# An encoder layer on one core: sums of squares, weight sums and the Fourier fold take other places in the order

## The chip, the cores and the metric

The kernel runs on 1 core of one Trainium2 chip. The metric is the device time of one execution in microseconds, lower is better. The engines are PE (TensorE, the matmuls), DVE (VectorE), ACT (ScalarE), POOL (GpSimd) and SP (SyncE, which issues most transfers). Each engine works through its own list in the order in which the program wrote it, and waits at an instruction until what it needs is there.

## The reference

One encoder layer for 1024 prompt tokens and 256 sample tokens, all in fp32:

```
trunk(x):
  xn = rms_norm(x);  h = xn @ w_in              # u_f 256, c_q 384, c_kv 256, k_rope 64
  y_f = real(fft2(u_f))                         # over tokens and over 4 groups of 64
  q  = rms_norm(c_q) @ w_q_up;  kv = rms_norm(c_kv) @ w_kv_up   # 6 heads
  y_a = softmax(q k^T) v                        # rope on a part of q and k
  x = x + concat(y_f, y_a) @ w_out
  x = x + (silu(rms_norm(x) @ w_gate) * (rms_norm(x) @ w_up)) @ w_down   # 2816 wide
  return rms_norm(x)
```

## The kernel before

The tokens lie in three chunks: 0 and 1 are the prompt (512 columns each), 2 is the sample (256). A matrix product runs as three fp32r passes over a high and a low part of both operands (mm3, L112). A high part is a copy by ACT (L93), a low part a subtraction by DVE or POOL (L98). The order on PE, ACT, DVE and POOL is written out by hand: nothing is moved by a scheduler, so a line that stands elsewhere in the program stands elsewhere in each engine's list. Buffers come from rotating pools, and a matmul waits until a PSUM bank is free (four banks of kind mm, two double banks sc).

A sum of squares over the 1024 rows is an accumulator on which POOL adds squares that ACT made. The class Rstd turns it into a reciprocal root: pre splits the accumulator (ACT high part, DVE low part, tile ssq), mid sums it over the partitions with two matmuls (L188, L189) and takes logarithm and exponential on ACT, post is four DVE operations (post_op 0 to 3, L208 to L215); post_op 0 is the last to read the bank.

Stages, with their places in the profiled execution:

- 0 to 124: phase_A projects a chunk into the latents, proj_U into u_f and k_rope, in the order chunk 0, 2, 1. x_pre, x_mid and x_post make the root of the input norm, c_pre, c_mid and c_post those of the two latent norms, c_norm scales a latent. rcols (L410) transposes the root of the input norm and is needed behind proj_U.
- 124 to 169: the queries (q_rope, whose result two to three DVE operations read out of the bank, L578 and L581; q_nope), first keys (kproj) and the latent norms of chunk 1. fold_U, on DVE, folds u_f for the Fourier transform: its first call is four additions (L391), each other call four more operations.
- 169 to 199: the first four score blocks (step), with queries and values between them. From 199 on the folded u_f is used; then the attention, to about 450.
- 450 to 570: the output projection (out_proj, index m from 0 to 7 per chunk), with squares for the second norm in hacc, one accumulator for each chunk.
- 570 to 1136: gate and up projections, for chunks 0 and 1 as a block scheme with seven products in place of eight: it needs sums of weight blocks (S1 to S4, made in prep from the raw weights) and sums of activation blocks (T1 to T4, from scaled, the normalised rows of chunk 1, L1111, and C0, those of chunk 0). The products are started by run in the order of seq; chunk 2 goes the plain way (rest). The first pair of weights (fp 0) has its own order: A11, A12, A21, A22 first, then S2, S1, S3, S4, A22.
- From 1136 on: the down projection and the last norm.

Of the kernel before, what the change touches and what calls it, by code (L numbers as in the profile page):

```python
# [35 lines left out]
def encoder_kernel(ctx, tc, A, out):  # L36
# [425 lines left out]
    def step0(k):  # L462
        if k + 2 < KD:
            load_w(k + 2)
            load_x(0, k + 2)
        if k + 1 < KD:
            split_w(k + 1, 0)
            split_x(0, k + 1, nc.vector)
        split_w(k, 1)
        if k == KD - 2:  # L470
            for kk in range(4):
                load_x(2, kk)
        if k == KD - 1:
            x_pre(0)
            for kk in range(4, KD):
                load_x(2, kk)

    phase_A(0, {k: (lambda k=k: step0(k)) for k in range(KD)})
    proj_U(0, 0)
    x_mid(0)  # L480
    x_post(0)
    late_consts()
    proj_U(0, 1)
# [3 lines left out]
    evac_U(0, 1)  # L487
    for k in range(KD):
        split_x(2, k, nc.vector)
    c_pre(0)  # L490
    proj_U(0, 2)
    evac_U(0, 2)
    proj_U(0, 3)
# [3 lines left out]
    def hooks2(k):  # L497
        load_x(1, k)
        if k == 0:
            x_pre(2)  # L500
        if k == 2:
            c_mid(0)
        if k == 3:
            c_post(0)
            x_mid(2)
        if k == 4:
            x_post(2)
        if k >= 3:
            c_norm(0, k - 3)

    phase_A(2, {k: (lambda k=k: hooks2(k)) for k in range(KD)})
    evac_A(2)
# [3 lines left out]
    rcols(2)  # L516
    evac_U(2, 0)
    c_pre(2)
    proj_U(2, 1)
    evac_U(2, 1)  # L520
    rope_k(2)
# [15 lines left out]
            x_pre(1)  # L537

    phase_A(1, {k: (lambda k=k: hooks1(k)) for k in range(KD)})
    proj_U(1, 0)  # L540
    x_mid(1)
    x_post(1)
    W.split(2)
    proj_U(1, 1)
# [414 lines left out]
    q_rope(0, 0)  # L959
    q_nope(0, 0)  # L960
    q_rope(0, 2)
    c_mid(1)
    q_nope(2, 0)
    q_rope(1, 0)
    cch[1][0].post()
    q_nope(0, 1)
    q_rope(1, 2)
    c_norm(1, 0)
# [15 lines left out]
    qsplit(0, 0, 0)  # L984
    qsplit(0, 0, 1)
    W.split(5)
    fold_U(0, nc.vector)
    q_nope(1, 1)
    q_rope(2, 1)
    fold_U(1, nc.vector)  # L990
    W.split(6)
    kr_transpose(1)
    q_nope(1, 2)
    kproj(0, 1)
    q_nope(2, 2)
    fold_U(2, nc.vector)
    fold_U(3, nc.vector)
    W.split(ib + 1)
    more = [(t, h) for h in range(3, H) for t in (0, 2, 1)]
    vp = [(t, j) for t in range(3) for j in range(TC[t][1] // P)]  # L1000
    for s in range(4):
        step(S[s], extra.get(s, ()))
        if s == 3:
            W.split(ib + 2)
            step(None)
        for a in more[9 * s // 4 : 9 * (s + 1) // 4]:
            q_nope(*a)
        vproj(0, *vp[s])
        if s == 0:
            fold_U(4, nc.vector)  # L1010
    W.split(ib + 3, 0)

    R, Rh = [], {}
# [119 lines left out]
        scaled(C0[m], m, 0)  # L1133

    def parts0(m):
        B["B21" if m > 3 else "B11"][m % 4] = split(pair(512, "b"), C0[m], nc.gpsimd if m > 3 else nc.vector)

    def plain2(m):

# [32 lines left out]
            src = A["w_up" if q % 2 else "w_gate"]  # L1172
            raws2[q] = [wload(src[f_ * P : (f_ + 1) * P, :], 1024) for f_ in (q // 2 * 2, q // 2 * 2 + 1)]

    def prep(upto, only_sums=False):


        while done[0] < min(upto, len(seq)):
            n = done[0]
            fp, k, name = seq[n]  # L1180
            q = 2 * fp + k
            load_pair(q)
            ra, rb = raws2[q]
            blk = {"A11": ra[:, :512], "A12": ra[:, 512:], "A21": rb[:, :512], "A22": rb[:, 512:]}
            blk |= {"S3": blk["A11"], "S1": blk["A21"], "S4": blk["A12"], "S2": sums.get(q)}
            eng = nc.vector if fp else nc.gpsimd

            def made(o, x, y, op):
                eng.tensor_tensor(blk[o], blk[x], blk[y], op=op)

            if name == "S2" and q not in sums:
                made("S3", "A11", "A21", ALU.subtract)
                made("S1", "A21", "A22", ALU.add)
                blk["S2"] = sums[q] = tmp([P, 512])
                made("S2", "A22", "S3", ALU.subtract)
                blk["S2"] = sums[q]
                if fp == 0:
                    made("S4", "A12", "S2", ALU.subtract)
            elif name == "S4" and fp:
                made("S4", "A12", "S2", ALU.subtract)  # L1200
            if only_sums:
                return
            if n % 2 == 0:
                piece["tile"] = wtile([P, 2, 2, 512], F32R, "wo")
            o = piece["tile"][:, n % 2]
            piece[n] = split((o[:, 0], o[:, 1]), blk[name], nc.gpsimd if n > 7 else nc.vector)
            done[0] += 1
            if name == "A22" and (fp or n > 8):
                load_pair(q + 2)

    state = {}

# [89 lines left out]
    for m in range(9):  # L1302
        W.split(min(io + 8 + m + 3, idn))
        if m == 6:
            prep(4)
        if m == 7:
            prep(8)
        if m < 8:
            load_res(m + 1, 1) if m < 7 else None
            load_res(m, 2)  # L1310
            out_proj(W.get(io + 8 + m), m, 1)
        if m == 7:
            hch[1] = Rstd(hacc[1], 512, D)
            hch[1].pre()
            prep(9, True)
        if m == 8:
            hch[1].mid()
        if m > 0:
            out_proj(W.get(io + 7 + m), m - 1, 2)
            plain2(m - 1)  # L1320
        if m == 0:
            hch[0].mid()
            hch[0].post()
        elif m < 5:
            chunk0(m - 1)
            chunk0(m + 3)
        for k in {4: (0,), 5: (1,), 6: (2,), 7: (3, 4, 5, 6, 7)}.get(m, ()):
            parts0(k)
        if m == 5:
            load_pair(0)  # L1330
            load_pair(1)
    hch[1].post()


    run(0)
# [2 lines left out]
        scaled(B["T3"][j][1], j, 1)  # L1338
        scaled(B["B22"][j][1], j + 4, 1)
    run(1)  # L1340
    hch[2] = Rstd(hacc[2], 256, D)
    hch[2].out = r2
    hch[2].pre()
    prep(10)

    def combine(o, x, y):
# [2 lines left out]
    for j in range(4):  # L1349
        ca, cb = B["T3"][j][1], B["B22"][j][1]  # L1350
        B["T1"][j] = low(C0.pop(j))
        combine(B["T1"][j][1], ca, B["T1"][j][1])
        B["T2"][j] = low(vtile([P, 512], F32, "c"))
        combine(B["T2"][j][1], cb, B["T1"][j][1])
    t4, t4r = wtile([P, 4, 512], F32R, "t4"), wtile([P, 4, 512], F32, "t4r")
    for j in range(4):
        B["T4"][j] = (t4[:, j], t4r[:, j])
        nc.gpsimd.tensor_tensor(t4r[:, j], C0.pop(j + 4), B["T2"][j][1], op=ALU.subtract)
    hch[2].mid()
    run(2)  # L1360
    run(3)
    split_block("T2", nc.vector)
# [269 lines left out]
```

## Time and profile before

| what | us |
|---|---|
| median of 3 runs (1460.93 to 1464.58) | 1461.56 |
| profiled execution, its own time | 1457.55 |
| its span, first to last instruction | 1455.3 |
| PE busy in the span | 1395.1 |
| DVE busy | 858.9 |
| POOL busy | 633.4 |
| ACT busy | 549.3 |

The profiled execution is one run and lies 4.0 us under the median. PE is busy for 96% of the span, the other engines for about half of it or less, so the view that matters is where PE stands still, and what ended each stop.

### The profile page before, as it was taken

The numbers are of one execution on the slowest core, as the hardware profiler recorded it, in microseconds if no ns is written. First come the engines' busy times: TensorE is split into PE (matmuls) and PEld (weight loads), VectorE is DVE, ScalarE is ACT, GpSimd is POOL, SyncE is SP. The second block draws the span as 40 slices with busy tenths as digits, with TensorE's granted clock in tenths as the row PEclk, the third lists the DMA queues.
The fourth block names the chain that finished last, engine by engine and source line by source line (L and its number), as shares of the span: only waits on it lengthen the run. The fifth ranks groups of instructions, "written<-read, shape, count | busy, mean of one in ns | idle before, by whom it ended". The sixth has DMA issues, their size and how long they took to land.

```text
span 1455.3 us, 27581 instructions
## 1 busy us (share of the span) xinstructions
PE 1395.1 (96%) x11096; PEld 1346.9 (93%) x11096; DVE 858.9 (59%) x1283; ACT 549.3 (38%) x1107; POOL 633.4 (44%) x452
## 2 busy tenths in 40 slices
PE   9999899999989998799999999999999999999997
PEld 8898797888869997799999999999999999999996
DVE  6867947898994677873243324333432467777434
ACT  5554346676774424242222222222123222113132
POOL 3455614453552555464444443534344142234333
PEclk9999999999999999899999999999999999999999
DMA  8103445686765552031212121212223543234002
GB/s 258 54 1 118 134 122 137 147 201 169 185 188 157 196 177 80 15 109 52 73 66 95 45 79 68 83 49 67 86 67 102 178 150 102 84 121 166 1 37 109
DMA packets 76192, 157.50 MB, mean 108 GB/s; under 512 B 13216, under 2 KB 23200, under 8 KB 75936
## 3 DMA queue, kind: packets, MB, share of 16 engines
q1 hardware_dynamic: 73008, 150.74, 33.9%
q10 hardware_dynamic: 2736, 3.95, 0.8%
q8 instruction: 87, 1.43, 0.4%
q0 software_dynamic: 320, 1.05, 0.2%
q14 instruction: 41, 0.34, 0.1%
HBM read 99.57 MB, written 35.16 MB: 93 GB/s over the span
## 4 chain that ended last, share of the span: by engine, by line
PE 80%; DVE 8%; issue 2%; ACT 2%; DMA 2%; POOL 1%; SPq 0%; DVEq 0%; ACTq 0%; POOLq 0%
PE mm L112 50%; PE sc L112 23%; PE sc L744 1%; PE sc L745 1%; PE sc L748 1%; PE sc L747 1%; PE sc L746 1%; DVE c L1111 1%; DVE mx L755 1%; DVE mx L98 1%; PE mm L821 1%; POOL whl L98 1%; DMA Y<-P 1%; DVE qw L581 0%; DVE at L98 0%
## 5 line engine op out<-in xcount | busy, mean ns | idle before, releaser
L112 PE MATMUL mm<-at,whl 128*128 128x256 f32 x2640 | 303.2, 277 | 4.8 <-DVE h L1426 2.3
L112 PEld LDWEIGHTS mm<-at,whl 128*128 128x128 f32 x2640 | 301.1, 188 | 6.2 <-DVE h L1426 2.9
L112 PE MATMUL sc<-b,wo 128*128 128x256 f32 x2288 | 292.0, 278 | 2.4 <-POOL wo L98 1.4
L112 PEld LDWEIGHTS sc<-b,wo 128*128 128x128 f32 x2288 | 275.9, 189 | 3.0 <-POOL wo L98 1.8
L98 POOL TENSOR_TENSOR wo<-wraw,wo 128x512 fp32r<-128x512 f32 x148 | 201.2, 1382 | 155.4 <-ACT wo L93 155.4
L1250 DVE TENSOR_TENSOR e<-e,sc 128x512 f32<-128x512 f32 x64 | 43.9, 688 | 225.5 <-PE sc L112 225.5
L1426 DVE TENSOR_TENSOR h<-h,mm 128x512 f32<-128x512 f32 (+1 forms) x192 | 111.7, 596 | 102.1 <-PE mm L112 101.6
L98 POOL TENSOR_TENSOR whl<-wraw,whl 128x1024 fp32r<-128x1024 f32 (+3 forms) x49 | 117.9, 2421 | 84.7 <-ACT whl L93 72.2
L112 PE MATMUL mm<-hn,wo 128*128 128x256 f32 x1056 | 130.3, 277 | 0.0
L112 PE MATMUL mm<-b,wo 128*128 128x256 f32 x1056 | 126.7, 276 | 0.0
L112 PEld LDWEIGHTS mm<-hn,wo 128*128 128x128 f32 x1056 | 125.0, 188 | 0.0
L112 PEld LDWEIGHTS mm<-b,wo 128*128 128x128 f32 x1056 | 123.0, 188 | 0.0
L112 PEld LDWEIGHTS mm<-mx,whl 128*128 128x128 f32 x960 | 111.2, 188 | 1.9 <-POOL whl L98 1.1
L112 PE MATMUL mm<-mx,whl 128*128 128x256 f32 x960 | 111.8, 278 | 0.9 <-POOL whl L98 0.9
L93 ACT ACTIVATE at<-araw 128x512 fp32r<-128x512 f32 x55 | 32.8, 624 | 159.7 <-DMA araw<-a 115.2
L93 ACT ACTIVATE wo<-wraw 128x512 fp32r<-128x512 f32 x156 | 87.8, 619 | 5.5 <-DMA wraw<-in_w_gate 4.1
L112 PE MATMUL mm<-pt,vt 128*128 128x512 f32 (+1 forms) x324 | 85.0, 400 | 4.2 <-DVE pt L98 3.9
L98 POOL TENSOR_TENSOR wo<-tmp,wo 128x512 fp32r<-128x512 f32 x22 | 29.3, 1333 | 134.2 <-ACT wo L93 134.2
L1439 POOL TENSOR_TENSOR h<-h,araw 128x512 f32<-128x512 f32 (+1 forms) x24 | 27.6, 1153 | 135.9 <-DVE h L1426 90.5
L98 POOL TENSOR_TENSOR pt<-wraw,pt 128x512 fp32r<-128x512 f32 x40 | 60.6, 1516 | 50.9 <-ACT pt L93 45.0
L1082 POOL TENSOR_TENSOR hacc<-hacc,tmp 128x512 f32<-128x512 f32 (+1 forms) x35 | 43.1, 1231 | 83.6 <-ACT tmp L1081 79.3
L112 PE MATMUL mm<-cn,whl 128*128 128x256 f32 x585 | 73.9, 283 | 5.2 <-DVE qw L581 3.5
(200 smaller groups left out, 2277.7 us busy)
## 6 DMA issues: line engine op xcount, KB each, us to landing
Y<-P SPq DMA_DIRECT2D x160, 128.0 KB, 2.6
wraw<-in_w_gate SPq DMA_DIRECT2D x22, 512.0 KB, 3.9
wraw<-in_w_up SPq DMA_DIRECT2D x22, 512.0 KB, 4.2
wraw<-in_w_down SPq DMA_DIRECT2D x22, 512.0 KB, 3.6
araw<-a SPq DMA_DIRECT2D x44, 256.0 KB, 4.5
a<-e SPq DMA_DIRECT2D x42, 256.0 KB, 2.0
araw<-in_x SPq DMA_DIRECT2D x32, 256.0 KB, 4.2
wraw<-in_w_out SPq DMA_DIRECT2D x16, 512.0 KB, 3.8
```

Source lines behind the costliest of these rows:

```text
L93: nc.scalar.activation(o, i, AF.Copy)
L98: eng.tensor_tensor(o, i, f(hi), op=ALU.subtract)
L112: nc.tensor.matmul(o[:, c], L[a], R[b][:, c], start=first and i == 0 and j == 0, stop=end, skip_group_check=again)
L744: nc.tensor.matmul(o, qn[0][:, cs], k[0], start=True, stop=False)
L745: nc.tensor.matmul(o, qn[0][:, cs], k[1], start=False, stop=False)
L746: nc.tensor.matmul(o, qn[1][:, cs], k[0], start=False, stop=False)
L747: nc.tensor.matmul(o, qr[0][:, cs], krst[kt], start=False, stop=False)
L748: nc.tensor.matmul(o, qr[1][:, cs], krst[kt], start=False, stop=True)
L1082: nc.gpsimd.tensor_tensor(acc[t], acc[t], q, op=ALU.add)
L1250: add = lambda o, x, y: nc.vector.tensor_tensor(o, x, y, op=ALU.add)
L1426: nc.vector.tensor_tensor(hview(m, t), hview(m, t), o, op=ALU.add)
L1439: nc.gpsimd.tensor_tensor(HV[m, t], HV[m, t], hres.pop((m, t)), op=ALU.add)
```

## The change

The change moves instructions, eight of them from POOL to DVE, and adds none. (1) x_mid stands ahead of the first proj_U for chunks 0 and 1. (2) In phase_A of chunk 2 the latent norm of chunk 0 comes later (c_mid at k = 4, c_pre inside the loop that splits chunk 2's input), and three of its five c_norm calls go behind that phase. (3) c_mid(1) comes one q_nope later and post_op 0 of both latent norms right behind it; fold_U goes from among the queries into the first three score blocks. (4) At the start of the feed-forward part all four sums of both weight blocks of the first pair are made on POOL by sums0 at m = 7, the low parts of B21 (parts0 4 to 7) go from POOL to DVE and ahead, chunk 2's root (hch[2].pre) is begun before run(0), and T4 is combined on DVE behind run(3), not on POOL before run(2).

```
     phase_A(0, ...)
+    x_mid(0)
     proj_U(0, 0)
-    x_mid(0)
...
         split_x(2, k, nc.vector)
-    c_pre(0)
+        if k == 4:
+            c_pre(0)
...
-        if k == 2:
-            c_mid(0)
         if k == 3:
-            c_post(0)
             x_mid(2)
         if k == 4:
             x_post(2)
-        if k >= 3:
-            c_norm(0, k - 3)
+            c_mid(0)
+        if k == 5:
+            c_post(0)
+        if k > 5:
+            c_norm(0, k - 6)
...
     c_pre(2)
+    for m in range(2, NPJ):
+        c_norm(0, m)
...
     phase_A(1, ...)
+    x_mid(1)
     proj_U(1, 0)
-    x_mid(1)
...
     q_rope(0, 2)
+    q_nope(2, 0)
     c_mid(1)
-    q_nope(2, 0)
+    for ch in cch[1]:
+        ch.post_op(0)
     q_rope(1, 0)
-    cch[1][0].post()
+    for i in range(1, 4):
+        cch[1][0].post_op(i)
...
-    fold_U(0, nc.vector)
     q_nope(1, 1)
     q_rope(2, 1)
-    fold_U(1, nc.vector)
...
-    fold_U(2, nc.vector)
-    fold_U(3, nc.vector)
...
-        if s == 0:
-            fold_U(4, nc.vector)
+        for q in ((0,), (1, 2), (3, 4), ())[s]:
+            fold_U(q, nc.vector)
...
-        B["B21" if m > 3 else "B11"][m % 4] = split(pair(512, "b"), C0[m], nc.gpsimd if m > 3 else nc.vector)
+        B["B21" if m > 3 else "B11"][m % 4] = split(pair(512, "b"), C0[m], nc.vector)
...
+    def sums0(q):
+        ra, rb = raws2[q]
+        sums[q] = tmp([P, 512])
+        a11, a12, a21, a22 = ra[:, :512], ra[:, 512:], rb[:, :512], rb[:, 512:]
+        for o, x, y, op in ((a11, a11, a21, ALU.subtract), (a21, a21, a22, ALU.add), (sums[q], a22, a11, ALU.subtract), (a12, a12, sums[q], ALU.subtract)):
+            nc.gpsimd.tensor_tensor(o, x, y, op=op)
...
         if m == 7:
             prep(8)
+            sums0(0)
+            sums0(1)
...
             hch[1].pre()
-            prep(9, True)
+            for k in range(4, 8):
+                parts0(k)
...
     hch[1].post()
+    hch[2] = Rstd(hacc[2], 256, D)
+    hch[2].out = r2
+    hch[2].pre()
     run(0)
...
     run(1)
-    hch[2] = Rstd(hacc[2], 256, D)
-    hch[2].out = r2
-    hch[2].pre()
     prep(10)
...
-        nc.gpsimd.tensor_tensor(t4r[:, j], C0.pop(j + 4), B["T2"][j][1], op=ALU.subtract)
     hch[2].mid()
     run(2)
     run(3)
+    raw2 = [c for _, c in B["T2"]]
     split_block("T2", nc.vector)
+    ...
+        combine(t4r[:, j], C0.pop(j + 4), raw2[j])
     hch[2].post()
```

DVE among the queries, from the first fold to the last key before the scores (fu, eu and E are the fold's tiles, qs and qw read a query out of its bank, krst and kn are key parts). Before:

```order
L391 TENSOR_TENSOR fu_2065<-U_583,U_1532 128x512
L391 TENSOR_TENSOR fu_2067<-U_669,U_1493 128x512
L391 TENSOR_TENSOR fu_2069<-U_583,U_1532 128x512
L391 TENSOR_TENSOR fu_2071<-U_1493,U_669 128x512
L578 TENSOR_TENSOR qs_2114<-mm_2095,rope_1647 128x512
L581 TENSOR_TENSOR qw_2116<-mm_2095,rope_1647 64x512 x2
L396 TENSOR_TENSOR eu_2124<-fu_2065,fu_2067 128x512
L397 TENSOR_TENSOR eu_2124<-U_583,U_1493 1x256
L402 CAST E_2127<-eu_2124 128x512
L98 TENSOR_TENSOR E_2127<-eu_2124,E_2127 128x512
L442 TENSOR_TENSOR krst_2140<-mm_2135,tmp_2142 64x512
L98 TENSOR_TENSOR kn_2181<-mm_2167,kn_2180 128x512
```

DVE at the same place after the change, up to the first addition of the fold (mx and nb are the maximum of a score block, vt a value part):

```order
L581 TENSOR_TENSOR qs_2106<-mm_2087,rope_1647 128x512
L584 TENSOR_TENSOR qw_2108<-mm_2087,rope_1647 64x512 x2
L442 TENSOR_TENSOR krst_2126<-mm_2121,tmp_2128 64x512
L98 TENSOR_TENSOR kn_2167<-mm_2153,kn_2166 128x512
L758 TENSOR_REDUCE mx_2199<-sc_2188 128x1
L760 TENSOR_SCALAR nb_2201<-mx_2199 128x1
L98 TENSOR_TENSOR vt_2251<-mm_2243,vt_2250 128x128
L98 TENSOR_TENSOR vt_2253<-mm_2243,vt_2252 128x128
L391 TENSOR_TENSOR fu_2258<-U_583,U_1532 128x512
```

The last query read (qs, qw) and both key parts now have no fold ahead of them; the fold begins behind the first block's maximum.

POOL around the last square sums of the output projection (hacc_6467 belongs to chunk 1, hacc_6573 to chunk 2; L1189 are weight sums, b the low parts of B21). Before:

```order
L1082 TENSOR_TENSOR hacc_6573<-hacc_6573,tmp_7081 128x256
L1082 TENSOR_TENSOR hacc_6467<-hacc_6467,tmp_7153 128x512
L1189 TENSOR_TENSOR wraw_6979<-wraw_6979,wraw_6981 128x512
L1189 TENSOR_TENSOR wraw_6981<-wraw_6981 128x512
L1189 TENSOR_TENSOR tmp_7163<-wraw_6981,wraw_6979 128x512
L1189 TENSOR_TENSOR wraw_6979<-wraw_6979,tmp_7163 128x512
L1082 TENSOR_TENSOR hacc_6573<-hacc_6573,tmp_7192 128x256
L98 TENSOR_TENSOR b_7203<-c_6580,b_7202 128x512
L98 TENSOR_TENSOR b_7207<-c_6679,b_7206 128x512
L98 TENSOR_TENSOR b_7211<-c_6778,b_7210 128x512
L98 TENSOR_TENSOR b_7215<-c_6876,b_7214 128x512
L1082 TENSOR_TENSOR hacc_6573<-hacc_6573,tmp_7251 128x256
```

POOL at the same place after the change (L1216 is sums0):

```order
L1085 TENSOR_TENSOR hacc_6573<-hacc_6573,tmp_7081 128x256
L1216 TENSOR_TENSOR wraw_6979<-wraw_6979,wraw_6981 128x512
L1216 TENSOR_TENSOR wraw_6981<-wraw_6981 128x512
L1216 TENSOR_TENSOR tmp_7105<-wraw_6981,wraw_6979 128x512
L1216 TENSOR_TENSOR wraw_6979<-wraw_6979,tmp_7105 128x512
L1216 TENSOR_TENSOR wraw_6983<-wraw_6983,wraw_6985 128x512
L1216 TENSOR_TENSOR wraw_6985<-wraw_6985 128x512
L1216 TENSOR_TENSOR tmp_7110<-wraw_6985,wraw_6983 128x512
L1216 TENSOR_TENSOR wraw_6983<-wraw_6983,tmp_7110 128x512
L1085 TENSOR_TENSOR hacc_6467<-hacc_6467,tmp_7167 128x512
L1085 TENSOR_TENSOR hacc_6573<-hacc_6573,tmp_7217 128x256
L1085 TENSOR_TENSOR hacc_6573<-hacc_6573,tmp_7256 128x256
```

Eight weight sums now stand ahead of chunk 1's last square sum, where four stood behind it; the four low parts between the last two additions for chunk 2 are gone from POOL.

DVE at the start of the feed-forward part (rstd is chunk 1's root, c a normalised row of chunk 1, ssq_7334 the split square sum of chunk 2). Before:

```order
L215 SCALAR_TENSOR_TENSOR rstd_7262<-ln_7221,r_1421_7223 128x512
L1111 SCALAR_TENSOR_TENSOR c_7291<-h_6465,gains,rstd_7262 128x512
L1111 SCALAR_TENSOR_TENSOR c_7292<-h_6836,gains,rstd_7262 128x512
L1111 SCALAR_TENSOR_TENSOR c_7295<-h_6465,gains,rstd_7262 128x512
L1111 SCALAR_TENSOR_TENSOR c_7296<-h_6836,gains,rstd_7262 128x512
L1111 SCALAR_TENSOR_TENSOR c_7299<-h_6465,gains,rstd_7262 128x512
L1111 SCALAR_TENSOR_TENSOR c_7300<-h_6836,gains,rstd_7262 128x512
L1111 SCALAR_TENSOR_TENSOR c_7303<-h_6465,gains,rstd_7262 128x512
L1111 SCALAR_TENSOR_TENSOR c_7304<-h_6836,gains,rstd_7262 128x512
L98 TENSOR_TENSOR ssq_7334<-hacc_6573,ssq_7334 128x256
```

DVE there after the change, its first five rows:

```order
L215 SCALAR_TENSOR_TENSOR rstd_7267<-ln_7226,r_1422_7228 128x512
L98 TENSOR_TENSOR ssq_7269<-hacc_6573,ssq_7269 128x256
L1114 SCALAR_TENSOR_TENSOR c_7299<-h_6465,gains,rstd_7267 128x512
L1114 SCALAR_TENSOR_TENSOR c_7300<-h_6836,gains,rstd_7267 128x512
L1114 SCALAR_TENSOR_TENSOR c_7303<-h_6465,gains,rstd_7267 128x512
```

The split of chunk 2's square sum stood behind the eight rows of chunk 1 and now stands ahead of them.

## Rows read from the trace of the kernel before

**Rows 1.** Windows: busy us of PE, PEld, DVE, ACT, POOL; PEclk, DMA, GB/s
```profile
150.00:175.00 25.00, 19.93 (x147) 18.63 (x145) 24.50 (x31) 8.48 (x14) 17.67 (x11) 0.93 0.49 147
...
575.00:600.00 25.00, 10.84 (x68) 10.34 (x67) 24.35 (x21) 7.31 (x13) 19.56 (x13) 0.66 0.02 6
...
650.00:675.00 25.00, 25.00 (x217) 25.00 (x217) 6.52 (x11) 7.88 (x14) 11.41 (x10) 1.00 0.18 59
```

**Rows 2.** PE's waits, 575 to 600: us in total, times, longest us
```profile
PE mm L189 <- DVE ssq L98: 10.5, 1, 10.5
...
PE mm L188 <- ACT ssq L93: 3.6, 1, 3.6
```

**Rows 3.** The windows view around the longest stop of PE, 2 us each
```profile
577.00:579.00 2.00, 0.00 (x0) 0.00 (x0) 1.93 (x3) 0.00 (x0) 2.00 (x2) 1.00 0.00 0
...
579.00:581.00 2.00, 0.58 (x1) 0.29 (x1) 2.00 (x3) 0.94 (x2) 0.95 (x2) 0.63 0.02 4
```

**Rows 4.** PE's waits, one row each of 25-50, 110-125 and 50-75
```profile
PE mm L410 <- DVE rstd L215: 0.6, 1, 0.6
...
PE mm L410 <- DVE rstd L215: 2.2, 1, 2.2
...
PE mm L189 <- DVE ssq L98: 2.0, 1, 2.0
```

**Rows 5.** Timeline, 45 to 75: start us, us, engine, line, operation, idle before
```profile
52.19 1.53 PE L112 MATMUL sc<-x,wA 128*128 128x256 f32 x12
...
59.72 0.41 DVE L98 TENSOR_TENSOR ssq<-xacc,ssq 128x256 fp32r<-128x256 f32 x1
```

**Rows 6.** PE's waits, 125 to 150
```profile
PE mm L112 <- DVE var L208: 0.8, 1, 0.8
...
PE mm L188 <- DVE qw L581: 0.7, 1, 0.7
```

**Rows 7.** PE's waits, 150 to 175
```profile
PE mm L112 <- DVE qw L581: 3.1, 1, 3.1
...
PE sc L745 <- DVE kn L98: 1.2, 1, 1.2
...
PE mm L112 <- DVE kn L98: 0.7, 1, 0.7
```

**Rows 8.** Timeline, 135 to 175: POOL's latent parts, the fold, PE behind it
```profile
145.87 3.41 POOL L98 TENSOR_TENSOR cn<-craw,cn 128x512 fp32r<-128x512 f32 x2
...
158.60 6.01 DVE L391 TENSOR_TENSOR fu<-U,U 128x512 f32<-128x512 f32 x4
...
166.76 2.26 PE L112 MATMUL mm<-cn,whl 128*128 128x256 f32 x9 [3.10 <-DVE qw L581]
```

**Rows 9.** Timeline, 555 to 630, in order of time
```profile
558.24 0.74 POOL L1082 TENSOR_TENSOR hacc<-hacc,tmp 128x256 f32<-128x256 f32 x1 [0.96 <-ACT tmp L1081]
...
565.40 1.27 POOL L1189 TENSOR_TENSOR wraw<-wraw,wraw 128x512 f32<-128x512 f32 x1
...
566.74 1.62 POOL L1189 TENSOR_TENSOR wraw<-wraw 128x512 f32<-128x512 f32 x1
...
567.27 0.50 PE L189 MATMUL mm<-ssq,ones_r 128*128 128x512 f32 x1 [0.62 <-DVE ssq L98]
...
570.43 5.82 PE L112 MATMUL sc<-b,wo 128*128 128x256 f32 x48
...
578.82 11.77 DVE L1111 SCALAR_TENSOR_TENSOR c<-h,gains,rstd 128x512 f32<-128x512 f32 x8
...
591.37 8.09 PE L112 MATMUL sc<-b,wo 128*128 128x256 f32 x48
...
616.42 2.50 DVE L1347 TENSOR_TENSOR c<-c,c 128x512 f32<-128x512 f32 x4
...
628.50 5.60 PE L112 MATMUL mm<-b,wo 128*128 128x256 f32 x48
```

More of the change, by code (lines that the diff above doesn't have):

```diff
@@ L972, in encoder_kernel @@
     c_norm(1, 2)
-    cch[1][1].post()
+    for i in range(1, 4):
+        cch[1][1].post_op(i)
     kproj(0, 0)
@@ L1173, in load_pair, with prep @@
             raws2[q] = [wload(src[f_ * P : (f_ + 1) * P, :], 1024) for f_ in (q // 2 * 2, q // 2 * 2 + 1)]
-    def prep(upto, only_sums=False):
+    def prep(upto):
         while done[0] < min(upto, len(seq)):
@@ L1185, in prep @@
             blk |= {"S3": blk["A11"], "S1": blk["A21"], "S4": blk["A12"], "S2": sums.get(q)}
-            eng = nc.vector if fp else nc.gpsimd
             def made(o, x, y, op):
-                eng.tensor_tensor(blk[o], blk[x], blk[y], op=op)
-            if name == "S2" and q not in sums:
+                nc.vector.tensor_tensor(blk[o], blk[x], blk[y], op=op)
+            if fp == 0:
+                pass
+            elif name == "S2":
                 made("S3", "A11", "A21", ALU.subtract)
@@ L1195, in prep @@
                 made("S2", "A22", "S3", ALU.subtract)
[L1196 to L1199, printed above, removed]
+            elif name == "S4":
                 made("S4", "A12", "S2", ALU.subtract)
-            if only_sums:
-                return
             if n % 2 == 0:
@@ L1326, in encoder_kernel @@
             chunk0(m + 3)
-        for k in {4: (0,), 5: (1,), 6: (2,), 7: (3, 4, 5, 6, 7)}.get(m, ()):
+        for k in {4: (0,), 5: (1,), 6: (2, 3)}.get(m, ()):
             parts0(k)
@@ L1354, in encoder_kernel @@
         combine(B["T2"][j][1], cb, B["T1"][j][1])
+    hch[2].mid()
+    run(2)
+    run(3)
+    raw2 = [c for _, c in B["T2"]]
+    split_block("T2", nc.vector)
     t4, t4r = wtile([P, 4, 512], F32R, "t4"), wtile([P, 4, 512], F32, "t4r")
@@ L1357, in encoder_kernel @@
         B["T4"][j] = (t4[:, j], t4r[:, j])
-        nc.gpsimd.tensor_tensor(t4r[:, j], C0.pop(j + 4), B["T2"][j][1], op=ALU.subtract)
[L1359 to L1362, printed above, removed]
+        combine(t4r[:, j], C0.pop(j + 4), raw2[j])
     hch[2].post()
```

## The prediction, made before the changed kernel ran

> **What bounds the kernel now.** I read the windows view first: where PE is busy in every microsecond, no other engine can give time back. In 650 to 675, a stretch like all those up to 1125, PE is busy for 25.00 of 25.00 at clock 1.00, so nothing there is to be had [rows 1]. In 575 to 600 it is busy for 10.84, the worst stretch of the trace, at a mean clock of 0.66, and in 150 to 175 for 19.93 at 0.93, while DVE is busy for over 24 in both [rows 1]. Then I read what ended PE's stops. In 575 to 600 two waits make 14.1 us, 3.6 and 10.5, both for chunk 2's split square sum [rows 2]; the clock, 1.00 in 577 to 579, is 0.63 over 579 to 581, so it fell during that stop [rows 3], and the 48 matmuls behind it took 8.09 where 48 of the same form took 5.82 before it [rows 9]: another 2.3 us. Among the queries PE waited 3.1, 1.2 and 0.7 [rows 7], 0.8 and 0.7 [rows 6], all for DVE. Ahead of them stand 0.6 and 2.2 for the transposed root and 2.0 for a latent norm's split [rows 4].
>
> **The change part by part.** The sum is made against the profiled execution's own 1457.55 us (its span of 1455.3 and 2.25 around it). That is 4.0 under the median of 1461.56, so I carry the difference over to the median.
>
> *x_mid ahead of proj_U.* The two matmuls only change places with proj_U. The root then has eight k steps of proj_U more to be made in (24 matmuls with 320 columns), so both waits for it should go: 0.6 and 2.2 [rows 4]. That needs the split square sum at the end of phase_A; if it were late, the same wait would come back ahead of proj_U, so the bounds are 0 and 2.8. I take 2.8, because PE did not wait for that split in either place.
>
> *The latent norm of chunk 0, later in phase_A of chunk 2.* The wait of 2.0 at k = 2 goes [rows 4]. But DVE is the late one here, and its list up to chunk 2's own split is the same set of operations. That split ends at 59.72 + 0.41 = 60.1 [rows 5]. PE starts the phase at 52.19 [rows 5]; without the stop it is at k = 3, where it needs the split, after 45 matmuls at 5.82/48 = 0.12, so at 57.6. Both move up by the 0.6, and PE waits 2.5 there. The stall goes from k = 2 to k = 3; I book 0. The bounds are a gain of 2.0 if DVE comes sooner, and a loss of 2 if the longer stop lets the clock fall. The three c_norm behind the phase delay DVE ahead of chunk 1's splits, which I count as hidden: PE needs these parts only from k = 2 of the next phase, at 24 matmuls of proj_U and more ahead.
>
> *Queries and fold.* The four additions of the first fold take 6.01 us on DVE, 1.5 each, and q_rope's bank is read only behind them [rows 8]. With the fold behind the first scores, the 3.1, 1.2 and 0.7 have no cause left [rows 7]: 5.0. With post_op 0 pulled ahead, two banks come free earlier, which ends the 0.8 and 0.7 [rows 6]: 1.5. The clock lost 0.07 of 25 us [rows 1], 1.75, mostly behind the 3.1 (nine matmuls took 2.26 there, 0.25 each [rows 8]); I take 1.5. Something else is late next: POOL finishes two low parts of chunk 1's latent at 145.87 + 3.41 = 149.3 [rows 8]; the root ahead of them comes about 2 earlier, PE reaches q_rope(0, 1) earlier by more, so I take off 1.2 as an estimate. Net 6.8. The fold itself is not free: it now lies on DVE between the score blocks, ahead of the next block's maximum. It is some 20 operations, 12 to 20 us by prices between 0.63 and 1.5, in about 30 us of PE work, and what is late next is the exponential of a block whose bank is wanted two blocks on. I book 0 there; with the bounds of no gain at all and the whole 8.3 the part is worth 0 to 8.3.
>
> *The feed-forward start, by the clock of the trace before.* POOL ends an addition at 558.24 + 0.74 = 559.0 and starts on the eight sums. One took 1.27 beside a quiet DVE and 1.62 beside a busy one [rows 9], so all take 10.2 to 13.0; I take 11.8, since the second waits for a low part. Only at 570.8 does chunk 1's last square sum follow, 1.3 more; before it ended at 565.4, 1.87 ahead of L189 at 567.27 [rows 9]. So L189 comes at about 573.9 and PE, which has the last piece of out_proj queued behind it, stands 6.4 longer there. That stop is about 8 us and should cost the 2.3 of a fallen clock. Then out_proj(7, 2), run(0) and run(1) end at 576.25 (570.43 + 5.82 [rows 9]) + 6.4 + 2.3 = 585.0. Chunk 2's split now stands right behind chunk 1's root on DVE, some 5 us after out_proj(7, 2) ends, so at 584.2: the wait of 14.1 and its 2.3 go. PE runs on with run(2), run(3), eight rest and four more run: 240 matmuls, 28 us at 5.60 for 48 [rows 9], up to 613.0.
>
> There it needs T3. DVE has, from 584.2 on, 34 operations of 128x512: eight rows, eight differences, four each for T2, T4 and T1, and six to combine products. Undisturbed they cost 2.50/4 = 0.63 [rows 9], 0.65 with the slower forms, 22.1; the last three of chunk 2's root add about 1.7. Beside POOL the eight rows took 11.77/8 = 1.47 each [rows 9], 0.84 more. POOL has only four low parts in this stretch now, so I add 4 x 0.84 = 3.4. DVE then starts T3's differences at 611.4, where it did at 616.42 [rows 9]. T3's parts and the S3 pieces behind them follow as before, PE waits for them some 2 us, and S4's products start 5.0 earlier than 628.50 [rows 9]. The part gives 5.0. Bounds: 10 if POOL never disturbs DVE, as then PE's 28 us are the limit, and a loss of 6 if half of the 34 run at 1.47 (14.3 in place of 3.4).
>
> The Trainium skill (SBUF — State Buffer, Who interferes with whom) says that a VectorE operation with two SBUF inputs and a GpSimd instruction that reads SBUF shut each other out for a whole instruction. By that rule the four low parts would hold DVE for their full 1.3 to 1.6 us, about 5.8 in place of 3.4, and the sum below would be 12.2 in place of 14.6. The rows show a mean of 0.84 per operation; no row here separates a single pair.
>
> **Sum.** 2.8 + 0 + 6.8 + 5.0 = 14.6: 1442.9 for a profiled execution, 1447 for the median.
>
> **The rivals.**
> *A, the forecast*, gain 11 to 19: 1442.5 to 1450.5.
> *B, the early sums eat the feed-forward gain.* For it: the late square sum is new, and everything on DVE hangs on it. Against it: 14.1 us of wait are there to pay with. Gain 2.8 + 6.8 = 9.6: 1452.
> *C, the gap closes nearly whole.* If the sums fit into time in which POOL stands still, or chunk 1's root is not late, the feed-forward part gives 12 and not 5. Against it: the order on POOL. Gain 22: 1440.
> *D, the moved fold holds up the score blocks* and eats the 6.8. For it: DVE is busy for 24.50 of 25 right there [rows 1]. Against: the fold's price fits. Gain 7.8: 1454. B and D together leave 2.8, within 0.3%: 1459.
> *E, slower: the sums on POOL put chunk 1's root so late that DVE's whole list shifts.* Place: POOL at 559. If each takes 1.62 (13.0), the addition behind them ends at 573.3, L189 comes at 575.2 and the root at about 587, and with all 34 operations at 1.47 (50.0) T3 starts at about 639, some 22 later than now. Less the 9.6 that is 12 slower, 1474. It decides from a T3 start at 630.4 on (616.42 plus the 9.6 and the 4.4 of 0.3%). Against it: POOL has too little left to disturb all 34.
>
> **How the numbers follow.** Within 0.3% (4.4 us) a measurement of this kernel can hardly be told from no change: the three runs span 3.65. Chances: A 0.50, B 0.19, C 0.13, D 0.08, B with D 0.06, E 0.04. So faster 0.90, same 0.06, slower 0.04. The range runs from inside C to past D, 1438 to 1455.5: it leaves out E, B with D, and the outer parts of C and D, about 0.18.
>
> **What would show it.** After the change, PE's wait at L410 is under 0.3 in both places; in phase_A of chunk 2 a wait of about 2.5 stands at chunk 2's L189, none at k = 2; PE has no wait over 1.5 between the first query and the first scores, and the granted clock there is 1.00. At the feed-forward start the wait at chunk 1's L189 (with L188) is about 8 us, that at chunk 2's is near 0, half clock follows the first, and a wait of 1 to 3 stands at the first product with T3. I am wrong if POOL makes the eight sums before PE reaches the first L189, if chunk 2's split is still late, or if new waits of PE appear among the score blocks or at the Fourier products.

## The result and the profile after

The changed kernel took 1451.45 us (median of ten executions, 1449.46 to 1457.92), the kernel before 1460.4 on the same chip; the ratio is 0.9938, with a 95% interval of 0.9920 to 0.9956. That is 9.0 us faster, give or take 2.6. I had forecast 14.6. The time lies inside the range, but outside the 1442.5 to 1450.5 of forecast A and nearest to rival B's 9.6; the runs below show how far B's way had a part in it. The profiled execution took 1450.82 (span 1449.0), only 6.7 under the profiled one of before.

PE's waits after, in stretches of 25 us that begin at 50, 125, 225, 550 and 600 (us in total, times, longest):

```profile
PE mm L189 <- DVE ssq L98: 1.7, 1, 1.7
PE mm L188 <- ACT ssq L93: 0.7, 1, 0.7
...
PE mm L112 <- ACT tmp L93: 1.8, 1, 1.8
...
PE mm L112 <- DVE pt L98: 3.8, 2, 1.9
...
PE mm L188 <- ACT ssq L93: 8.8, 1, 8.8
...
PE sc L112 <- ACT wo L93: 2.5, 1, 2.5
PE sc L112 <- POOL wo L98: 1.6, 1, 1.6
```

Both waits at L410 of [rows 4] have no row any more, and 14.1 of [rows 2] and the 3.1 of [rows 7] are gone. In their place stand 8.8 for chunk 1's square sum, 2.5 and 1.6 at the first product with T3, and a second wait for pt (the transposed probabilities). The windows view of after (columns as in [rows 1]):

```profile
50.00:75.00 25.00, 22.64 (x167) 21.84 (x166) 20.53 (x35) 13.38 (x32) 11.74 (x14) 0.93 0.10 30
...
150.00:175.00 25.00, 24.77 (x193) 23.55 (x192) 16.05 (x23) 12.25 (x24) 16.73 (x12) 1.00 0.57 175
...
525.00:550.00 25.00, 25.00 (x215) 25.00 (x214) 15.67 (x19) 9.37 (x17) 11.54 (x8) 1.00 0.45 140
550.00:575.00 25.00, 16.25 (x119) 15.51 (x118) 13.18 (x17) 9.66 (x19) 15.30 (x12) 0.80 0.08 27
575.00:600.00 25.00, 25.00 (x215) 25.00 (x214) 23.51 (x31) 9.99 (x18) 7.14 (x5) 1.00 0.14 54
600.00:625.00 25.00, 20.25 (x157) 19.44 (x157) 19.85 (x34) 13.34 (x25) 10.84 (x6) 0.93 0.16 50
```

The worst stretch of before, 10.84 busy, is full; the one ahead of it now lacks 8.75, and the clock is under 1.00 in three of these stretches. Before reading on, one row of before for the same out_proj matmuls as the third row above:

```profile
525.00:550.00 25.00, 25.00 (x223) 25.00 (x222) 16.44 (x16) 8.19 (x15) 14.15 (x9) 1.00 0.44 139
```

PE never stops in either, at clock 1.00, and yet 223 matmuls lie in one and 215 in the other. I call this the **pace**: in the trace the starts of such matmuls stand 113.3 or 117.8 ns apart, for a long stretch at a time, and it is another from execution to execution (last section). To compare stages I take it out: stage length, less the excess of each start-to-start distance over 113.33 ns (226.67 for 512 columns). Stages run from the first product of one kind to the next; "booked" is the share of the forecast:

| stage, pace taken out | before | after | won | booked |
|---|---|---|---|---|
| up to phase_A of chunk 2 | 51.2 | 50.8 | 0.5 | 0.6 |
| phase_A of chunk 2 | 17.6 | 19.1 | -1.5 | 0 |
| on to the first query | 53.7 | 51.2 | 2.5 | 2.2 |
| queries to the first Fourier product | 73.6 | 67.0 | 6.5 | 6.8 |
| score blocks, to out_proj | 244.9 | 246.6 | -1.7 | 0 |
| out_proj to the first product with T4 | 185.9 | 183.2 | 2.7 | 5.0 |
| the rest | 817.1 | 817.5 | -0.3 | 0 |

The sum is 8.7; the pace takes 2.35 more in after's execution (13.72 against 11.37), which leaves the 6.3 between the spans. So 8.7 agrees with the medians' 9.0, and the three rows with the wrong booking are where to look. Each figure is of one execution, though, and where DVE's list and not PE sets the time, a slow pace costs nothing, so that taking it out flatters the kernel that had it (see e2).

The timeline of after at the feed-forward start (columns as in [rows 5]):

```profile
554.30 1.50 POOL L1216 TENSOR_TENSOR wraw<-wraw,wraw 128x512 f32<-128x512 f32 x1
...
557.70 1.60 POOL L1216 TENSOR_TENSOR wraw<-wraw 128x512 f32<-128x512 f32 x1 [1.90 <-DVE wo L98]
...
567.75 1.26 POOL L1085 TENSOR_TENSOR hacc<-hacc,tmp 128x512 f32<-128x512 f32 x1
...
569.72 0.79 PE L188 MATMUL mm<-ssq,ones_r 128*128 128x512 f32 x1 [8.76 <-ACT ssq L93]
...
575.20 5.82 PE L112 MATMUL sc<-b,wo 128*128 128x256 f32 x48
...
580.35 7.45 DVE L1114 SCALAR_TENSOR_TENSOR c<-h,gains,rstd 128x512 f32<-128x512 f32 x8
...
582.25 3.02 POOL L98 TENSOR_TENSOR wo<-tmp,wo 128x512 fp32r<-128x512 f32 x2 [5.09 <-ACT wo L93]
...
593.63 4.69 DVE L98 TENSOR_TENSOR b<-c,b 128x512 fp32r<-128x512 f32 x4
...
594.38 3.39 POOL L98 TENSOR_TENSOR wo<-wraw,wo 128x512 fp32r<-128x512 f32 x2 [9.12 <-ACT wo L93]
...
609.26 2.49 DVE L1357 TENSOR_TENSOR c<-c,c 128x512 f32<-128x512 f32 x4
...
613.05 0.74 PE L112 MATMUL sc<-b,wo 128*128 128x256 f32 x4 [2.48 <-ACT wo L93]
...
615.35 6.68 PE L112 MATMUL sc<-b,wo 128*128 128x256 f32 x44 [1.56 <-POOL wo L98]
```

The eight sums keep POOL from 554.30 to the 567.75 of the addition behind them, 13.5 us, with a hole of 1.90 in which the second waits for a low part on DVE; the square sum's addition comes only behind them. DVE's list then runs from 580.35 to 609.26, 28.9 us.

Theory one, formed here: the feed-forward part loses against its booking because POOL's rows hold up PE once (ahead of the square sum) and DVE twice (low parts beside c and b, each of which costs DVE more than the 0.84 that I took). Rival: DVE's list is as long as PE's work whoever does the rest. For the early part: the fold's price in the score blocks (rival D), against a chance of clock and order.

### The profile page after: what moved, and what is told of

Read it like the earlier page. It is cut to its first block, busy times and chain, and to the rows that moved or that the text cites. A ratio compares the mean times of both kernels' runs of the same rounds, so it can differ in the third digit from the quotient of the medians.

```text
span 1449.0 us, 27553 instructions
## 1 busy us (share of the span) xinstructions
PE 1396.8 (96%) x11096; PEld 1350.2 (93%) x11096; DVE 851.4 (59%) x1291; ACT 548.7 (38%) x1107; POOL 616.8 (43%) x444
## 3 DMA queue, kind: packets, MB, share of 16 engines
q8 instruction: 87, 1.43, 0.4%
## 4 chain that ended last, share of the span: by engine, by line
PE 78%; DVE 10%; issue 3%; ACT 3%; POOL 2%; DMA 1%; SPq 0%; ACTq 0%; DVEq 0%; POOLq 0%
PE mm L112 49%; PE sc L112 22%; PE sc L747 1%; PE sc L748 1%; PE sc L751 1%; PE sc L750 1%; PE sc L749 1%; DVE mx L758 1%; DVE b L98 1%; DVE mx L98 1%; PE mm L824 1%; DVE c L1114 1%; POOL wo L98 0%; DVE at L98 0%; DVE wraw L818 0%
## 5 line engine op out<-in xcount | busy, mean ns | idle before, releaser
L112 PEld LDWEIGHTS mm<-mx,whl 128*128 128x128 f32 x960 | 114.3, 191 | 2.2 <-POOL whl L98 1.5
L112 PE MATMUL mm<-mx,whl 128*128 128x256 f32 x960 | 115.0, 281 | 1.1 <-POOL whl L98 0.9
L112 PEld LDWEIGHTS mm<-pt,vt 128*128 128x128 f32 x324 | 57.2, 191 | 19.3 <-DVE pt L98 7.6
```

The costliest lines, as they stand in the source:

```text
L112: nc.tensor.matmul(o[:, c], L[a], R[b][:, c], start=first and i == 0 and j == 0, stop=end, skip_group_check=again)
```

## The experiments

**Early part alone** (e1): before, with the hunks of the change that stand ahead of `parts0` in its diff, and none of the others.

> The kernel before with only the early part of the change: the root's transposes, the latent norms, the queries' order and the moved fold; the feed-forward part is as before. By the prediction 9.6 us faster than before (2.8 and 6.8, and nothing lost elsewhere): a ratio of 0.9934. By the reading of the trace after, 2.8 and some 6.3 are won, and 1.5 is lost again to half clock in phase_A of chunk 2 and 1.5 to new waits among the score blocks: 6.1, a ratio of 0.9958. By rival D, under 3. In the rows: matmuls at half clock right behind chunk 2's square sum in phase_A, and waits of 3 to 5 for pt and P in 225 to 250, by the reading; neither, by the prediction.

Measured 0.9928 (0.9908 to 0.9948), 10.5 us faster. With the pace out: 3.2 won up to the queries, none lost in phase_A of chunk 2 (17.6), 5.9 won from the queries to the first Fourier product, 2.0 lost among the score blocks. The early part holds its 9.6 within the interval; the loss among the score blocks is there, the half clock in phase_A is not. In time, the early part alone cannot be told from the whole change (0.9920 to 0.9956).

**Feed-forward part alone** (e2): before, with the other hunks, from `parts0` on.

> The kernel before with only the feed-forward part of the change. By the prediction 5.0 faster (ratio 0.9966): a stop of about 8 at chunk 1's square sum, none at chunk 2's, T3's differences 5 earlier. By the reading of the trace after, about 3.3 (0.9977), since DVE's list takes 28.9 in place of 27.2 and the first product with T3 then waits 2.5 for ACT and 1.6 for POOL, which lets the clock fall once more. By rival B, about 0. The stop at chunk 1's square sum should be 8 to 9 by all three.

Measured 0.9976 (0.9960 to 0.9992), 3.5 faster; with the pace out the stage from out_proj on takes 185.4 in place of 185.9. Up to out_proj the kernel is the one of before, and runs 0.5 behind it here: POOL's last addition ahead of the sums ends at 558.76 + 0.74 = 559.5, in before at 559.0 [rows 9].

```profile
558.76 0.74 POOL L1082 TENSOR_TENSOR hacc<-hacc,tmp 128x256 f32<-128x256 f32 x1 [0.96 <-ACT tmp L1081]
...
575.58 0.79 PE L189 MATMUL mm<-ssq,ones_r 128*128 128x512 f32 x1
...
580.67 5.60 PE L112 MATMUL sc<-b,wo 128*128 128x256 f32 x48
...
585.83 7.46 DVE L1111 SCALAR_TENSOR_TENSOR c<-h,gains,rstd 128x512 f32<-128x512 f32 x8
...
614.76 2.49 DVE L1354 TENSOR_TENSOR c<-c,c 128x512 f32<-128x512 f32 x4
...
618.55 0.73 PE L112 MATMUL sc<-b,wo 128*128 128x256 f32 x4 [0.87 <-ACT wo L93]
...
620.85 6.86 PE L112 MATMUL sc<-b,wo 128*128 128x256 f32 x44 [1.57 <-POOL wo L98]
...
627.54 5.60 PE L112 MATMUL mm<-b,wo 128*128 128x256 f32 x48
```

I had L189 at 573.9, T3's differences at 611.4, S4's products at 623.5. By the clock of before they come at 575.1, 614.2 and 627.0: 1.2 late at L189, 2.8 at T3, 3.5 at S4. Of the 5.0 there is 1.5 left, and most of that is pace.

From run(0) to T3's differences this run takes 614.76 - 580.67 = 34.09 us, the changed kernel 609.26 - 575.20 = 34.06, and e4, e5, e7 and e8 the same within 0.03, although the pace adds 1.08 us to the matmuls of this stretch in after and 0.02 here. DVE's list sets its length, and the 2.7 in the table holds 1.1 that was not won. With the pace taken out only up to run(0), the stage takes 186.1 in before and in e1, 184.2 in after, and 185.3 to 185.6 in e2, e4, e7 and e8, which have the same code there: 0.4 to 1.9 are won. The whole times are less sharp. The 5.0 lies inside the interval here, and the two parts make 10.5 + 3.5 = 14.0 where the whole change makes 9.0, each give or take 2.3 to 2.9; whether more than chance parts the two sums no run shows.

**Sums in two pieces behind the square sums** (e3):

```
-            sums0(0)
-            sums0(1)            # ahead of out_proj(7, 1)
+            sums0(0)            # behind chunk 1's hch[1].pre()
+    sums0(1)                    # behind out_proj(7, 2)
```

> The changed kernel with the eight early sums on POOL moved: four right behind chunk 1's last square sum, four behind chunk 2's. Everything else is the changed kernel's. If it is the sums ahead of the square sum that hold PE up (the prediction's step for the 6.4), the wait of 8.8 at chunk 1's square sum falls under 2, the half clock behind it goes, and T3's differences start at about 603 in place of 609.3: 4 to 7 faster than the changed kernel, a ratio to before near 0.990. By the rival that DVE's list bounds this stretch and the sums only move beside DVE's rows, where each costs it about 1.2, less than 2 is won: 0.993.

Measured 0.9919 (0.9894 to 0.9944). The interval holds both 0.990 and 0.993. The stop at chunk 1 falls to 1.1 and 0.6, but the stage takes 183.1, as in after (184.0 with the pace taken out up to run(0); 184.2 in after, 185.3 to 185.6 in the other executions of that code): the sums now lie beside DVE's rows, and DVE pays.

```profile
562.03 5.78 DVE L98 TENSOR_TENSOR b<-c,b 128x512 fp32r<-128x512 f32 x4
...
578.22 0.58 PE L189 MATMUL mm<-ssq,ones_r 128*128 128x256 f32 x1 [5.86 <-DVE ssq L98]
...
606.99 2.49 DVE L1357 TENSOR_TENSOR c<-c,c 128x512 f32<-128x512 f32 x4
```

The four b took 5.78 in place of 2.49, the stop moved to chunk 2, T3 came at 607.0, not 603 (605.8 by after's clock, since out_proj begins 1.2 later here). By the stage, at most 1.6 is won: that is the rival's outcome, though not yet its reason.

**Fold back in its old places** (e4), the rest as changed:

```
     W.split(5)
+    fold_U(0, nc.vector)
...
+    fold_U(1, nc.vector)        # behind q_rope(2, 1); 2 and 3 behind q_nope(2, 2)
...
-        for q in ((0,), (1, 2), (3, 4), ())[s]:
-            fold_U(q, nc.vector)
+        if s == 0:
+            fold_U(4, nc.vector)
```

> The changed kernel with the Fourier fold back at its four places among the queries; the rest of the queries' new order stays. By the prediction the waits of 3.1, 1.2 and 0.7 and the half clock behind the first come back: 5 to 6.5 slower than the changed kernel, a ratio to before near 0.997. By the reading of the trace after, that is partly paid back, because the waits for pt and P in 225 to 250 fall from 4.6 to about 2: 4 to 5 slower than the changed kernel. If the new order of the banks alone had ended the waits, there would be no difference to the changed kernel.

Measured 0.9936 (0.9919 to 0.9952), in time not to be told from the change; the expected 0.997 lies outside. With the pace out, queries and first scores take 73.1 (67.0 after, 73.6 before): the waits of 2.6 and 1.1 are back, so in this execution the new order of the banks alone wins 0.5 and the fold's move all else. That these 6.1 do not show in the whole times is not explained by any run. The score blocks take 245.8, 0.8 less than after, and the second wait for pt is down to 0.3: the fold's move costs something there.

**Sums one step of out_proj earlier** (e5):

```
         if m == 6:
-            prep(4)
+            prep(8)             # and sums0(0) behind out_proj(6, 1)
         if m == 7:
-            prep(8)
-            sums0(0)
             sums0(1)
```

> The changed kernel with the second half of the first pair's weight splits made one step of out_proj earlier, four of the eight sums right behind the step m = 6 of chunk 1, four ahead of m = 7. If it is the sums in front of the last square sum that hold PE up and the sums beside DVE's rows that stretch DVE's list, both go: the stop at chunk 1's square sum falls from 8.8 to about 1.5, the half clock behind it goes, T3's differences start near 598 in place of 609.3 and nothing waits for them: 8 to 10 faster than the changed kernel, a ratio to before near 0.988. By the rival, the sums beside out_proj's own rows hold back the weight parts of the last steps and PE waits there instead: 3 or less.

Measured 0.9956 (0.9938 to 0.9973), in time not to be told from the change, and the stop got longer, the rival's way:

```profile
551.69 1.15 ACT L93 ACTIVATE wo<-wraw 128x512 fp32r<-128x512 f32 x2 [3.49 <-PE mm L112]
...
570.38 0.80 PE L188 MATMUL mm<-ssq,ones_r 128*128 128x512 f32 x1 [10.25 <-ACT ssq L93]
```

ACT's copy of the last weight tile waited 3.49 for PE, which I take for the wait for a free buffer; DVE stood behind it, and the addition of m = 6 came to POOL only at 555.2. All eight sums still lie ahead of the last square sum, now for 10.2 us.

**Low parts of S2 and S1 on DVE** (e6), one execution:

```
-            piece[n] = split(..., nc.gpsimd if n > 7 else nc.vector)
+            piece[n] = split(..., nc.gpsimd if n > 11 else nc.vector)
```

> The changed kernel with the four low parts of the first two pairs of sums (S2 and S1) on DVE in place of POOL. If a POOL row that lies beside DVE's holds DVE for its whole length less a little (1.16 us each by the rows of after: 7.45 for the eight c and 4.69 for the four b), DVE gets 4.65 back and pays 4 times 0.65: T3's differences start about 2 earlier than in the changed kernel, measured from the first product of the feed-forward network. By the prediction's mean of 0.84 the four cost 3.4 and it is 0.8 earlier.

From run(0) to T3's differences it is 605.03 - 573.02 = 32.0, against 609.26 - 575.20 = 34.1 in the changed kernel: 2.05 earlier, with four more rows on DVE. The c without a POOL row beside them took 5.38 in place of 7.45, the b 2.50 in place of 4.69. The mean of 0.84 was too small; it is 1.0 to 1.1 for each POOL row (2.07 and 2.19, two rows each).

**Low parts of pt on DVE** (e7), one execution:

```
-            sub_lo(nc.gpsimd if b.moved and kc % 2 else nc.vector, pt[1], src, pt[0])
+            sub_lo(nc.vector, pt[1], src, pt[0])
```

> The changed kernel with every low part of the transposed probabilities on DVE; 40 of them were on POOL. If the waits of 1.85 and 1.91 for pt in 225 to 232 come from POOL and DVE starting on their two low parts in the same tenth of a microsecond, so that DVE's takes 1.7 in place of 0.69, both waits fall under 0.7 and the score blocks get 2 to 3 shorter. By the theory that the moved fold is what is late there, the second wait stays. By the rival that DVE is full in this stretch, its 40 more rows (some 28 us) bring new waits and the score blocks get longer by several us.

The longest wait for pt in 225 to 250 is 1.2, so the two of 1.9 are gone, but the score blocks take 251.2 in place of 246.6: DVE is full. What decided the second wait can be seen in two pairs of rows, of after first:

```profile
229.14 1.26 POOL L98 TENSOR_TENSOR pt<-wraw,pt 128x512 fp32r<-128x512 f32 x1 [0.62 <-DVE mx L758]
229.18 1.77 DVE L98 TENSOR_TENSOR pt<-wraw,pt 128x512 fp32r<-128x512 f32 x1
...
231.01 1.43 PE L112 MATMUL mm<-pt,vt 128*128 128x512 f32 x5 [1.91 <-DVE pt L98]
```

and of before:

```profile
234.26 2.09 PE L112 MATMUL mm<-pt,vt 128*128 128x512 f32 x5 [1.86 <-DVE pt L98]
...
236.66 0.69 DVE L98 TENSOR_TENSOR pt<-wraw,pt 128x512 fp32r<-128x512 f32 x1
236.74 1.76 POOL L98 TENSOR_TENSOR pt<-wraw,pt 128x512 fp32r<-128x512 f32 x1 [0.74 <-DVE nb L757]
```

In both pairs the row that starts second is held until the other has ended: 0.69 becomes 1.77, or 1.26 becomes 1.76. In before DVE was first by 0.08 us and PE did not wait; in after POOL is first by 0.04 and PE waits 1.91. Not all of the 1.91 is a loss, however: in before the clock fell behind the first wait (0.93 over 225 to 250, in after 1.00), and five products took 2.09 in place of 1.43. From the first product with pt to the next scores of 512 columns before needs 239.12 - 232.01 = 7.11 us and after 232.27 - 224.48 = 7.79, so 0.7 is lost. These are single pairs, which I said no row showed, and they agree with the Trainium skill (SBUF — State Buffer, Who interferes with whom): each shuts the other out for a whole instruction.

**Latent norm of chunk 0 in its old places** (e8), one execution: the hunks of the change at `c_pre(0)`, in `hooks2` and behind `c_pre(2)` taken back.

> The changed kernel with chunk 0's latent norm back in its old places in phase_A of chunk 2 and ahead of it. By the prediction (nothing won or lost by that edit) the stop of 2.0 to 2.5 moves back from k = 3 to k = 2 and the phase takes as long as in the changed kernel. By the reading that the half clock behind the stop is what made the phase 19.1 in place of 17.6, and that the stop's new form brings it, it takes 17.6 again.

```profile
PE mm L189 <- DVE ssq L98: 2.0, 1, 2.0
PE mm L188 <- DVE krw L361: 0.3, 1, 0.3
...
57.00:59.00 2.00, 1.84 (x10) 1.76 (x11) 1.91 (x7) 1.94 (x4) 0.78 (x1) 0.76 0.00 0
59.00:61.00 2.00, 2.00 (x11) 2.00 (x11) 1.93 (x4) 0.48 (x1) 1.27 (x2) 0.50 0.00 0
```

The waits are those of before, yet here the clock is 0.50 over 59 to 61, and the phase takes 19.2. With the old order it took 17.6 twice and 19.2 once; with the new one 17.4 to 17.7 in eight runs and 19.1 to 19.2 in three (after, e3, e4). My reading fell: both orders are followed by half clock in some executions, and nothing shows that the new one brings it. The booking of 0 was right; after's 1.5 is half clock behind a stop of 2.4, which in eight other runs of the same order did not come.

**Sums on DVE** (e9, all eight behind chunk 1's split), **low parts there too** (e10), and **S3's parts ahead of T3's differences** (e11):

```
-            nc.gpsimd.tensor_tensor(o, x, y, op=op)     # in sums0
+            nc.vector.tensor_tensor(o, x, y, op=op)     # e9, e10 (n > 11 as in e6), e11 (n > 13)
     run(9)
+    prep(14)                                            # e11, from behind split_block("T3")
```

> The changed kernel with the eight early sums on DVE in place of POOL, right behind chunk 1's last split. If POOL's rows beside DVE's are what stretched DVE's list in the run with the sums in two pieces (sums 10.4 us on POOL, some 6.8 lost on DVE), the same sums on DVE cost 8 times 0.65 = 5.2 and nothing beside them: chunk 1's stop stays under 2, the stop at chunk 2's square sum is about 4 in place of 5.9, and from the first product of out_proj to the first with T4 the kernel needs 4 to 6 less than the changed one's 186.9. By the rival, that DVE's list is as long as PE's work here whoever makes the sums, it needs 2 less at most.

> The same, with the four low parts of S2 and S1 on DVE too, so that POOL has nothing left beside DVE's list up to T3. By whole instructions of POOL that hold DVE (4.65 lost for the four, 2.6 paid) T3's differences start about 2 earlier again, counted from chunk 1's square sum; by the prediction's mean of 0.84, 0.8 earlier. The ratio to before should be near 0.988 by the first, and 0.990 by the second.

> The same, with the two weight parts of S3 made ahead of T3's differences, low parts on DVE. In the changed kernel the first product with T3 waited 2.5 for ACT, which made T3's four high parts first, and 1.6 for POOL's low part. If those two waits are what is late there, both go and the clock stays up: 2 to 4 faster than the run without this edit. If T3 itself is late, the wait only changes its name and nothing is won.

Measured 0.9895 (0.9869 to 0.9922), 0.9881 (0.9851 to 0.9912) and 0.9876 (0.9847 to 0.9905). The stage takes 180.3, 178.3 and 178.4 with the pace out, against 183.2. One row tells e9 from e10, the last of chunk 1's root, first beside a POOL row, then alone:

```profile
572.42 2.98 POOL L98 TENSOR_TENSOR wo<-tmp,wo 128x512 fp32r<-128x512 f32 x2 [2.02 <-ACT wo L93]
572.64 1.64 DVE L215 SCALAR_TENSOR_TENSOR rstd<-ln,r 128x512 f32<-128x512 f32 x1
```

```profile
573.39 0.69 DVE L215 SCALAR_TENSOR_TENSOR rstd<-ln,r 128x512 f32<-128x512 f32 x1
...
601.20 2.49 DVE L1357 TENSOR_TENSOR c<-c,c 128x512 f32<-128x512 f32 x4
```

From chunk 1's split to T3's differences e9 needs 44.1 and e10 42.1: 2.0 earlier again. e9 itself won 2.9 against after, between the two expectations (3.7 with the pace taken out up to run(0), and about 5 against the other executions of the changed code): the stop at chunk 2 is 2.8 and 4.4. In e11 the first product with T3 waits 0.6 in place of 2.5 in sum, but nothing is won: with two more low parts ahead of them T3's differences come 43.3 behind chunk 1's split in place of 42.1, and the next DVE rows meet POOL:

```profile
607.24 6.37 POOL L98 TENSOR_TENSOR wo<-wraw,wo 128x512 fp32r<-128x512 f32 x4 [37.16 <-ACT wo L93]
607.35 6.80 DVE L98 TENSOR_TENSOR b<-c,b 128x512 fp32r<-128x512 f32 x4
```

**All of it, with DVE's list reordered** (e12), low parts on DVE up to A22 (n > 17):

```
             sums0(0)
-            sums0(1)
-            for k in range(4, 8):
-                parts0(k)
...
     hch[2].pre()
+    for k in range(4, 8):
+        parts0(k)
+    sums0(1)
```

> The run before this one, with the four parts of B21 and the second four sums put behind chunk 2's split on DVE, and the low parts of S4 and A22 on DVE as well. By the theory that DVE's list is what bounds the stretch up to T3, the stops at chunk 2's square sum (3.2 and 2.4) fall under 1 in sum and the half clock behind them goes, but T3's differences still start about 43 behind chunk 1's square sum, so PE waits there instead: from the first product of out_proj to the first with T4 it needs 1 to 3 less than the 178.9 of the run before, and the ratio to before is near 0.987. By the rival that PE's stops are what is lost, 5 to 7 less, 0.983.

Measured 0.9888 (0.9866 to 0.9911). The stage takes 175.6, 2.8 less than e11, as the list theory has it; the stop at chunk 2 is 0.5, and PE waits for T2 in its place:

```profile
571.66 0.38 PE L189 MATMUL mm<-ssq,ones_r 128*128 128x256 f32 x1 [0.51 <-DVE ssq L98]
...
598.53 0.50 PE L112 MATMUL mm<-b,wo 128*128 128x256 f32 x2 [3.29 <-ACT b L93]
```

e10, e11 and e12 cannot be told apart in time. All three beat both kernels: about 17 us under before, where the change is 9.

## Why the prediction was right or wrong

**The sum**: the range holds 1451.45 because it is 17.5 us wide and reaches past B and D; the forecast itself was 1447, and B's 1452 is 0.55 away. What happened lies between A and B, as the last paragraphs of this section show. The half clock in phase_A, which cost 1.5 in the profiled execution, came in 3 of 11 runs of that order: chance, as far as they show. The new wait among the score blocks is one of the signs of being wrong that the prediction names.

**x_mid ahead of proj_U**: right. 2.8 booked, 2.8 to 3.6 won up to the queries in the runs whose clock held up to there.

**The latent norm of chunk 0**: right to book 0. The stall went from k = 2 to k = 3, with 0.7 and 1.7 for the 2.5. The bound of a loss by half clock came true in after, 1.5; e1, e8 and the rest show that the edit does not decide it.

**Queries and fold**: 6.8 booked, 6.5 won among the queries, clock 1.00 there. The wait of 1.8 that took the place of others was priced at 1.2, but it is another one: PE waited for ACT's copy out of a bank (the row with tmp in the first view of the result), not for POOL's two low parts. Wrong was the 0 for the score blocks: 0.9 to 2.7 were lost there in the runs with the fold moved (rival D, at 0.4 of its size or less), and 0.9 in e4, where it was not. One wait of 1.91, 0.7 of it a loss, is shown, by the order of two rows 0.04 us apart. Why POOL comes first in those runs is not shown; nor is the rest.

**The feed-forward start**: this is the term of the sum that was mis-sized. The mechanism is as written: a stop of 8.8 for "about 8", half clock behind it, none at chunk 2's split, and a wait at the first product with T3. Three terms were too good. "I take 11.8" for the eight sums measured 13.5, with the 1.90 hole. "4 x 0.84 = 3.4" for POOL's low parts beside DVE measured 2.07 and 2.19, 4.3 (e6): a mean over the eight rows of [rows 9] hides how many of them were held. And behind T3 I let the S3 pieces "follow as before"; PE waited 4.0 there in after, and the clock fell once more. 5.0 booked, 1.9 in after, 0.4 to 0.8 in e2, e4, e7 and e8: most of the gain was eaten, as rival B had it, though by three costs and not by the early sums alone. By the rule of the Trainium skill (SBUF — State Buffer, Who interferes with whom) I had put the low parts' term at 5.8; the 4.3 lies between the two, and the single pairs of e7 agree with the rule.

The waits of before were 14.1 there; the change removed them and won 1.9 at most. The rest became the stop at chunk 1, and that stop is POOL's order: e3 removes it and wins 0.2 against after and 1.6 at most while POOL still works beside DVE; e9 and e10 take POOL's rows away and win 2.9 and 4.8 against after, and the whole time follows (0.9881 in e10, its interval clear of the change's). DVE's list is the bound that is left, as far as the one profiled execution of e12 shows it; in time e12 is no faster than e10.

## What to carry to other kernels

Moving element-wise work to the idle engine was the dear choice here: the eight sums kept POOL for 13.5 us, held PE for 8.8 behind them, or (in e3) four rows of DVE for 3.3; DVE made all eight itself in 5.4 (558.94 to 564.34 in e9). Price a row on one of the two engines by what lies beside it on the other, pair by pair, and not by a mean. When a gain of a stage is booked, walk on to the next two products behind it: a stop that goes usually comes back there in part. And take executions apart by stage before you compare them: here two spans differ by as much from the pace alone as from a part of the change.

## What was not expected of the hardware

PE's pace at full clock has two values. The same products of the last matrix in before and in e3, 1200 to 1225:

```profile
1200.00:1225.00 25.00, 25.00 (x223) 25.00 (x222) 18.67 (x28) 4.20 (x6) 8.04 (x5) 1.00 0.27 85
```

```profile
1200.00:1225.00 25.00, 25.00 (x215) 25.00 (x214) 16.30 (x26) 4.27 (x7) 7.67 (x5) 1.00 0.37 122
```

Both are without a stop and at clock 1.00, with starts 113.3 and 117.8 ns apart in the mean; over the stage that these products make up it is 6.5 of 6.7 us (327.9 against 321.2), more than most terms of the sum. The code there is the same in all runs and shows either value: 215 also in e1, e2, e6 and e9, 223 in the others. What sets it is open. It may be much of the 4 to 13 us by which single executions of one kernel differ; that share was not measured.
